# Cross-covariance attention on one core: two heads per step in 256-byte runs, or units of four heads in 1 KB runs with a written-out pipeline

## The chip, the cores and the metric

The kernel runs on one core of one Trainium2 chip. The number that is compared is the device time of one execution in microseconds (us), the median of several. The core has TensorE (matrix products, PE in the rows), VectorE (DVE), ScalarE (ACT), GpSimd (POOL), SyncE (SP, which here only issues DMAs), and 16 DMA engines that move data between HBM and the on-chip memory SBUF. TensorE writes its products to PSUM, which VectorE and ScalarE can read.

## What is computed

Q, K and V have the shape (8, 12, 512, 64): 96 heads, each of 512 tokens by 64 channels, in float32. The norms and the first product run over the tokens, so that the attention matrix of a head is only 64x64:

```python
Q_norm = Q / (np.linalg.norm(Q, axis=-2, keepdims=True) + 1e-10)
K_norm = K / (np.linalg.norm(K, axis=-2, keepdims=True) + 1e-10)
attn = np.einsum('bhnd,bhne->bhde', Q_norm, K_norm)
attn = np.exp(attn - np.max(attn, axis=-1, keepdims=True))
attn = attn / (np.sum(attn, axis=-1, keepdims=True) + 1e-10)
return np.einsum('bhnd,bhde->bhne', V, attn)
```

Both kernels leave out the subtraction of the maximum, since the logits are cosines. The three inputs and the output are 12.58 MB each, 50.33 MB in all.

## The kernel before, in words

The 512 tokens of a head are cut as (t p): token 128*t + p lies in partition p. So a partition holds, per head, four rows of 64 floats that lie 32 KB apart in HBM, and each run of contiguous bytes of a transfer is 256 B. The loop takes two heads per step, 48 steps. A step loads Q, K and V of two heads (three DMAs of 256 KB, lines 52 to 54) and casts them to bf16: VectorE writes Q and K side by side into `qkb` (lines 57 and 58), ScalarE casts V (line 60).

Then for each of the two heads: four matmuls with `qkb` as both operands accumulate the 128x128 Gram matrix of [Q K] (line 67). Its diagonal holds the squared norms of all 128 channels; the block of rows 0 to 63 and columns 64 to 127 holds the unscaled logits. VectorE takes the diagonal by a multiplication with the identity and a sum (line 71). ScalarE takes the square root (line 76), VectorE the reciprocal (line 78). TensorE transposes this column to a row (line 81), VectorE copies it (line 83), TensorE forms the outer product of the two halves of the row, a 64x64 matrix of scales (line 86), and VectorE multiplies the logits by it (lines 88 and 90). ScalarE takes the exponential with its row sums (line 93), VectorE the reciprocal of the sums (line 95) and the normalised bf16 matrix (line 97). Four transposes turn V (line 101), ScalarE copies them out of PSUM (line 103), four matmuls form the output (line 107) and VectorE copies it out (line 108). Behind the second head, one DMA stores both (line 110).

The square root and the exponential need different tables on ScalarE, and a table load stands in the instruction stream where they alternate. A planner orders the instructions by costs of its own; big tiles have two buffers, small ones three, and the PSUM tiles of lines 81, 86 and 107 have one. All DMAs, loads and stores, stand in SyncE's one queue in program order.

Of the kernel before, what the change touches and what calls it, by code (L numbers as in the profile page):

```python
# [1 line left out]

# [6 lines left out]

F32 = mybir.dt.float32  # L10
BF16 = mybir.dt.bfloat16
AF = mybir.ActivationFunctionType
ALU = mybir.AluOpType


@with_exitstack
def kernel(
    ctx: ExitStack,
    tc: tile.TileContext,
    Q: bass.AP,  # L20
    K: bass.AP,
    V: bass.AP,
    out: bass.AP,
):
    nc = tc.nc
    B, H, N, D = Q.shape
    assert D == 64 and N % 128 == 0
    NT = N // 128
    BH = B * H
    BB = 2  # L30

    Qf = Q.rearrange("b h (t p) d -> (b h) p t d", p=128)
    Kf = K.rearrange("b h (t p) d -> (b h) p t d", p=128)
    Vf = V.rearrange("b h (t p) d -> (b h) p t d", p=128)
    Of = out.rearrange("b h (t p) d -> (b h) p t d", p=128)

    const = ctx.enter_context(tc.tile_pool(name="const", bufs=1))
    ident = const.tile([128, 128], F32)
    make_identity(nc, ident)
    identb = const.tile([128, 128], BF16)  # L40
    nc.vector.tensor_copy(identb, ident)

    sb = ctx.enter_context(tc.tile_pool(name="sb", bufs=2))
    sb_small = ctx.enter_context(tc.tile_pool(name="sb_small", bufs=3))
    ps = ctx.enter_context(tc.tile_pool(name="ps", bufs=2, space=bass.MemoryType.PSUM))
    ps_sm = ctx.enter_context(tc.tile_pool(name="ps_sm", bufs=1, space=bass.MemoryType.PSUM))

    for bh0 in range(0, BH, BB):
        qf = sb.tile([128, BB, NT, 64], F32)
        kf = sb.tile([128, BB, NT, 64], F32)  # L50
        v = sb.tile([128, BB, NT, 64], F32)
        nc.sync.dma_start(out=qf, in_=Qf[bh0:bh0 + BB].rearrange("g p t d -> p g t d"))
        nc.sync.dma_start(out=kf, in_=Kf[bh0:bh0 + BB].rearrange("g p t d -> p g t d"))
        nc.sync.dma_start(out=v, in_=Vf[bh0:bh0 + BB].rearrange("g p t d -> p g t d"))

        qkb = sb.tile([128, BB, NT, 128], BF16)
        nc.vector.tensor_copy(qkb[:, :, :, 0:64], qf)
        nc.vector.tensor_copy(qkb[:, :, :, 64:128], kf)  # L58
        vb = sb.tile([128, BB, NT, 64], BF16)
        nc.scalar.copy(vb, v)  # L60

        so = sb.tile([128, BB, NT, 64], F32)

        for g in range(BB):
            gram = ps.tile([128, 128], F32)
            for i in range(NT):
                nc.tensor.matmul(gram, qkb[:, g, i, :], qkb[:, g, i, :], start=(i == 0), stop=(i == NT - 1))  # L67

            gi = sb_small.tile([128, 128], F32)
            nsq = sb_small.tile([128, 1], F32)  # L70
            nc.vector.tensor_tensor_reduce(  # L71
                out=gi, in0=gram, in1=ident, scale=1.0, scalar=0.0,
                op0=ALU.mult, op1=ALU.add, accum_out=nsq,
            )
            nrm = sb_small.tile([128, 1], F32)
            nc.scalar.sqrt(nrm, nsq)  # L76
            invn = sb_small.tile([128, 1], F32)
            nc.vector.reciprocal(invn, nrm)  # L78

            invnT_p = ps_sm.tile([1, 128], F32)  # L80
            nc.tensor.transpose(invnT_p, invn, ident)  # L81
            invnT = sb_small.tile([1, 128], F32)
            nc.vector.tensor_copy(invnT, invnT_p)  # L83

            scale2 = ps_sm.tile([64, 64], F32)
            nc.tensor.matmul(scale2, invnT[0:1, 0:64], invnT[0:1, 64:128])  # L86
            attn_raw = sb_small.tile([64, 64], F32)
            nc.vector.tensor_copy(attn_raw, gram[0:64, 64:128])  # L88
            attn = sb_small.tile([64, 64], F32)
            nc.vector.tensor_mul(attn, attn_raw, scale2)  # L90

            rsum = sb_small.tile([64, 1], F32)
            nc.scalar.activation(attn, attn, AF.Exp, accum_out=rsum)  # L93
            rinv = sb_small.tile([64, 1], F32)
            nc.vector.reciprocal(rinv, rsum)  # L95
            attnb = sb_small.tile([64, 64], BF16)
            nc.vector.tensor_scalar(attnb, attn, rinv, None, op0=ALU.mult)  # L97

            vt_p = ps.tile([64, NT, 128], BF16)
            for i in range(NT):  # L100
                nc.tensor.transpose(vt_p[:, i, :], vb[:, g, i, :], identb)  # L101
            vt = sb.tile([64, NT, 128], BF16)
            nc.scalar.copy(vt, vt_p)  # L103

            po = ps_sm.tile([128, NT, 64], F32)
            for i in range(NT):
                nc.tensor.matmul(po[:, i, :], vt[:, i, :], attnb)  # L107
            nc.vector.tensor_copy(so[:, g, :, :], po)  # L108

        nc.sync.dma_start(out=Of[bh0:bh0 + BB].rearrange("g p t d -> p g t d"), in_=so)  # L110


# [1 line left out]
_INS = ['Q', 'K', 'V']  # L114
_OUTS = [((8, 12, 512, 64), 'float32')]


# [23 lines left out]
```

## Time and profile before

| | |
|---|---|
| median of 3 runs | 349.55 us (349.44 to 349.60) |
| span of the profiled execution, first to last instruction | 347.9 us |
| median less this span | 1.65 us |
| busy: ScalarE / TensorE / VectorE / GpSimd | 247.0 / 209.6 / 193.3 / 0.7 us |
| busy share of the 16 DMA engines | 71.7% |
| DMA traffic | 50.34 MB in packets of 256 B, mean 145 GB/s |

The profiled execution has no time of its own beside its span; the 1.65 us are what the timed runs take outside the first and last instruction. Busy time is time in which the engine executed something. None of the shares says alone what sets the end; for that the profile has a chain of waits, followed back from the last instruction, and lists of who waited for whom.

### The profile page before, as it was taken

The page shows a single profiled execution, that of the slowest core. Times are in us where ns is not written, and L with a number is a line of the kernel's source. Part 1 is how long each engine was busy: PE and PEld are TensorE (multiplying, and loading weights), DVE is VectorE, ACT ScalarE, POOL GpSimd, SP SyncE. Part 2 cuts the span into 40 slices and gives each one's busy share as a digit, 9 for nine tenths or more (in the row PEclk, how much of TensorE's full clock was granted, in tenths as well). Part 3 has the DMA queues.
Part 4 walks back from the last instruction along what each step waited for, and adds up shares of the span by engine and source line. Part 5 has one row for each costly group of instructions (what it writes and reads, how often), then busy time and mean ns, then how long its engine had stood idle before and what let it go on. Part 6 is the DMA issues. An engine that isn't in the chain of part 4 may idle for free.

```text
span 347.9 us, 4965 instructions
## 1 busy us (share of the span) xinstructions
PE 209.6 (60%) x1440; PEld 133.9 (38%) x1440; DVE 193.3 (56%) x961; ACT 247.0 (71%) x529; POOL 0.7 (0%) x6
## 2 busy tenths in 40 slices
PE   2866656567556656665655764675566565576463
PEld 1534334334334334443433433443334343344242
DVE  2765556555556555645655555655565565465553
ACT  4887768758767786685875877668677687677763
POOL 0000000000000000000000000000000000000000
DMA  9787697498668768669748876786965984787642
GB/s 176 136 170 143 136 187 141 95 188 170 124 133 163 168 134 159 131 129 194 152 92 170 167 148 121 157 167 134 180 121 121 190 168 100 157 166 159 123 90 60
DMA packets 199706, 50.65 MB, mean 146 GB/s; under 512 B 199680, under 2 KB 199680, under 8 KB 199680
## 3 DMA queue, kind: packets, MB, share of 16 engines
q1 hardware_dynamic: 199680, 50.34, 71.7%
q8 instruction: 11, 0.18, 0.2%
q14 instruction: 15, 0.12, 0.1%
HBM read 37.75 MB, written 12.58 MB: 145 GB/s over the span
## 4 chain that ended last, share of the span: by engine, by line
PE 44%; DVE 31%; ACT 12%; issue 10%; DMA 1%; SPq 0%; ACTq 0%
PE vt_p L101 12%; DVE so L108 10%; PE po L107 9%; PE invnT_p L81 8%; PE scale L86 8%; PE gram L67 7%; ACT L93 5%; DVE gi L71 5%; ACT vt L103 4%; DVE attnb L97 3%; DVE rinv L95 3%; DVE qkb L58 2%; DVE attn_raw L88 2%; DVE invnT L83 2%; ACT attn L93 2%
## 5 line engine op out<-in xcount | busy, mean ns | idle before, releaser
L103 ACT COPY vt<-vt_p 64x512 bf16<-64x512 bf16 x96 | 54.1, 574 | 50.1 <-PE vt_p L101 50.1
L107 PE MATMUL po<-attnb,vt 64*128 64x64 bf16 x384 | 35.7, 230 | 70.2 <-DVE rinv L95 47.4
L67 PE MATMUL gram<-qkb 128*128 128x128 bf16 x384 | 52.1, 310 | 25.3 <-DVE qkb L58 25.3
L93 ACT ACT_TABLE_LOAD x48 | 61.6, 1283 | 2.4 <-DVE attn L90 1.6
L76 ACT ACT_TABLE_LOAD x48 | 61.6, 1283 | 0.9
L101 PE MATMUL vt_p<-identb,vb 128*64 128x128 bf16 x384 | 56.3, 313 | 0.4 <-DVE nsq L71 0.4
L107 PEld LDWEIGHTS <-vt 64*128 64x128 bf16 x384 | 23.3, 115 | 86.2 <-ACT attn L93 56.0
L108 DVE COPY so<-po 128x256 f32<-128x256 f32 x96 | 40.6, 423 | 26.9 <-PE po L107 25.3
L81 PE MATMUL invnT_p<-ident,invn 128*1 128x128 f32 x96 | 35.8, 373 | 29.4 <-DVE invn L78 29.4
L90 DVE TENSOR_TENSOR attn<-attn_raw,scale 64x64 f32<-64x64 f32 x96 | 20.5, 213 | 57.1 <-PE scale L86 56.7
L86 PE MATMUL scale<-invnT 1*64 1x64 f32 x192 | 45.3, 337 | 9.2 <-DVE invnT L83 8.9
L67 PEld LDWEIGHTS <-qkb 128*128 128x128 bf16 x384 | 37.1, 139 | 33.7 <-DVE qkb L58 31.2
L101 PEld LDWEIGHTS <-vb 128*64 128x64 bf16 x384 | 38.7, 163 | 16.3 <-issue 10.3
L76 ACT ACTIVATE nrm<-nsq 128x1 f32<-128x1 f32 x96 | 19.1, 201 | 29.1 <-DVE nsq L71 27.9
L83 DVE COPY invnT<-invnT_p 1x128 f32<-1x128 f32 x96 | 26.7, 278 | 22.0 <-PE invnT_p L81 16.0
L86 PEld LDWEIGHTS scale<-invnT 1*64 1x64 f32 x192 | 27.3, 201 | 29.4 <-DVE invnT L83 21.5
L71 DVE CUSTOM_DVE_ANT_0 gi<-gram,ident 128x128 f32<-128x128 f32 x96 | 27.5, 286 | 17.0 <-PE gram L67 16.8
L60 ACT CAST vb<-v 128x512 bf16<-128x512 f32 x48 | 28.9, 602 | 4.4 <-DMA v<-in_V_dram 4.4
L93 ACT ACTIVATE attn<-attn 64x64 f32<-64x64 f32 x96 | 24.0, 250 | 8.3 <-DVE attn L90 7.8
L95 DVE RECIPROCAL rinv<-rsum 64x1 f32<-64x1 f32 x96 | 14.3, 149 | 19.7 <-ACT attn L93 19.7
L81 PEld LDWEIGHTS invnT_p<-ident,invn 128*1 128x1 f32 x96 | 7.6, 79 | 44.4 <-DVE invn L78 37.6
L97 DVE TENSOR_SCALAR attnb<-attn,rinv 64x64 bf16<-64x64 f32 x96 | 23.4, 244 | 2.2
(14 smaller groups left out, 100.2 us busy)
## 6 DMA issues: line engine op xcount, KB each, us to landing
qf<-in_Q_dram SPq DMA_DIRECT2D x48, 256.0 KB, 4.5
kf<-in_K_dram SPq DMA_DIRECT2D x48, 256.0 KB, 4.3
v<-in_V_dram SPq DMA_DIRECT2D x48, 256.0 KB, 4.2
out_dram<-so SPq DMA_DIRECT2D x48, 256.0 KB, 3.0
```

Source lines behind the costliest of these rows:

```text
L67: nc.tensor.matmul(gram, qkb[:, g, i, :], qkb[:, g, i, :], start=(i == 0), stop=(i == NT - 1))
L71: nc.vector.tensor_tensor_reduce(out=gi, in0=gram, in1=ident, scale=1.0, scalar=0.0, op0=ALU.mult, op1=ALU.add, accum_out=nsq,)
L76: nc.scalar.sqrt(nrm, nsq)
L81: nc.tensor.transpose(invnT_p, invn, ident)
L83: nc.vector.tensor_copy(invnT, invnT_p)
L86: nc.tensor.matmul(scale2, invnT[0:1, 0:64], invnT[0:1, 64:128])
L93: nc.scalar.activation(attn, attn, AF.Exp, accum_out=rsum)
L97: nc.vector.tensor_scalar(attnb, attn, rinv, None, op0=ALU.mult)
L101: nc.tensor.transpose(vt_p[:, i, :], vb[:, g, i, :], identb)
L103: nc.scalar.copy(vt, vt_p)
L107: nc.tensor.matmul(po[:, i, :], vt[:, i, :], attnb)
L108: nc.vector.tensor_copy(so[:, g, :, :], po)
```

## The change

The kernel is written anew round units of four heads (24 units; a unit is two pairs, PU = 2).

- **Layout.** Tokens are cut as (p t): token 4*p + t lies in partition p. A partition's four rows of a head are then contiguous in HBM, in runs of 1 KB. Each load or store moves four heads, 512 KB. Q and K of the same token still meet in the same partition, and the sums over tokens don't depend on their order.
- **Order.** The planner is switched off and instructions are issued as written. In step s SyncE issues the loads of unit s + 3 and the store of unit s - 6; the compute engines do the Gram matrices and norms of unit s, logits and exponentials of s - 1, the transposes of V of s, the casts of s + 1, the normalisation of s - 1, the scaling of s, the outputs of s - 2. Loads have five buffers, outputs ten. The last four stores stand behind the loop.
- **Casts.** All on VectorE, five per unit. In every second head Q and K change places in `qkb`, so that Q of an even head and Q of the odd one lie in different halves.
- **Norms.** Four masked sums over the PSUM blocks per unit give one column of squared norms for the 128 Q channels of a pair and one for the K channels. GpSimd raises them to the power -0.5 in one instruction on 128x4 values: no square root on ScalarE, no reciprocal, no transposed norms.
- **Logits.** K's factor is a per-partition scalar on the K-by-Q blocks (`scale_k`, which also zeroes the other blocks); a float32 matmul with two stacked identities transposes them to Q-by-K for two heads at a time; Q's factor is the scale of the exponential.
- **Output.** The normalised matrices of two heads stand as a block diagonal 128x128 matrix, V is transposed for two heads at a time, and one matmul gives two heads for 128 tokens: eight per unit. ScalarE copies the transposed V and the outputs out of PSUM.

The diff, without the lines removed:

```diff
--- before.py
+++ after.py
@@ -4,13 +4,17 @@
 import concourse.tile as tile
 from concourse import bass_utils, mybir
 from concourse._compat import with_exitstack
...
 from concourse.masks import make_identity
 F32 = mybir.dt.float32
 BF16 = mybir.dt.bfloat16
 AF = mybir.ActivationFunctionType
 ALU = mybir.AluOpType
+D = 64
+T = 4
+HU = 4
+PU = HU // 2
 @with_exitstack
@@ -23,91 +27,184 @@
     out: bass.AP,
 ):
     nc = tc.nc
...
+    B, H, N, _ = Q.shape
+    assert N == 128 * T and Q.shape[3] == D
     BH = B * H
...
+    U = BH // HU
+    Qf = Q.rearrange("b h (p t) d -> p (b h) t d", p=128)
+    Kf = K.rearrange("b h (p t) d -> p (b h) t d", p=128)
+    Vf = V.rearrange("b h (p t) d -> p (b h) t d", p=128)
+    Of = out.rearrange("b h (p t) d -> p (b h) t d", p=128)
+    ctx.enter_context(tc.manual_schedule())
     const = ctx.enter_context(tc.tile_pool(name="const", bufs=1))
...
+    qp = ctx.enter_context(tc.tile_pool(name="qp", bufs=5))
+    vp = ctx.enter_context(tc.tile_pool(name="vp", bufs=5))
+    vbp = ctx.enter_context(tc.tile_pool(name="vbp", bufs=3))
+    qkp = ctx.enter_context(tc.tile_pool(name="qkp", bufs=4))
+    vtp = ctx.enter_context(tc.tile_pool(name="vtp", bufs=4))
+    sop = ctx.enter_context(tc.tile_pool(name="sop", bufs=10))
+    small = ctx.enter_context(tc.tile_pool(name="small", bufs=4))
+    ps_g = ctx.enter_context(tc.tile_pool(name="ps_g", bufs=2, space=bass.MemoryType.PSUM))
+    ps_v = ctx.enter_context(tc.tile_pool(name="ps_v", bufs=2, space=bass.MemoryType.PSUM))
+    ps_l = ctx.enter_context(tc.tile_pool(name="ps_l", bufs=2, space=bass.MemoryType.PSUM))
+    ps_o = ctx.enter_context(tc.tile_pool(name="ps_o", bufs=2, space=bass.MemoryType.PSUM))
+    LOAD_AHEAD = 3
+    CAST_AHEAD = 1
+    STORE_LAG = 6
+    qf, kf, vf, vb, qkb, gram, nsq, kqs, rq, lg, ex, ab, vt, so = ({} for _ in range(14))
+    def load_qk(u):
+        qf[u] = qp.tile([128, HU, T, D], F32, name="qf")
+        kf[u] = qp.tile([128, HU, T, D], F32, name="kf")
+        nc.sync.dma_start(out=qf[u], in_=Qf[:, u * HU:(u + 1) * HU])
+        nc.sync.dma_start(out=kf[u], in_=Kf[:, u * HU:(u + 1) * HU])
+    def load_v(u):
+        vf[u] = vp.tile([128, HU, T, D], F32, name="vf")
+        nc.sync.dma_start(out=vf[u], in_=Vf[:, u * HU:(u + 1) * HU])
+    def store(u):
+        nc.sync.dma_start(out=Of[:, u * HU:(u + 1) * HU], in_=so[u])
+    def casts(u):
+        t_ = qkb[u] = qkp.tile([128, HU, T, 2 * D], BF16, name="qkb")
+        nc.vector.tensor_copy(t_[:, 0::2, :, 0:D], qf[u][:, 0::2])
+        nc.vector.tensor_copy(t_[:, 1::2, :, D:2 * D], qf[u][:, 1::2])
+        nc.vector.tensor_copy(t_[:, 0::2, :, D:2 * D], kf[u][:, 0::2])
+        nc.vector.tensor_copy(t_[:, 1::2, :, 0:D], kf[u][:, 1::2])
+        w = vb[u] = vbp.tile([128, T, HU, D], BF16, name="vb")
+        nc.vector.tensor_copy(w.rearrange("p t h d -> p h t d"), vf[u])
+    def grams(u):
+        g = gram[u] = ps_g.tile([128, PU, 4, D], F32, name="gram")
+        for h in range(HU):
+            o = g[:, h // 2, 2 * (h % 2):2 * (h % 2) + 2, :]
+            for t in range(T):
+                x = qkb[u][:, h, t, :]
+                nc.tensor.matmul(o, x, x, start=(t == 0), stop=(t == T - 1))
+    def norms(u):
+        n2 = nsq[u] = small.tile([128, 2, PU], F32, name="nsq")
+        for p in range(PU):
+            for c, (blk, m) in enumerate(((gram[u][:, p, 0::3, :], mask_q), (gram[u][:, p, 1:3, :], mask_k))):
+                scr = small.tile([128, 2, D], F32, name="scr")
+                nc.vector.tensor_tensor_reduce(
+                    out=scr, in0=blk, in1=m, scale=1.0, scalar=1e-20,
+                    op0=ALU.mult, op1=ALU.add, accum_out=n2[:, c, p:p + 1],
+                )
+        r = rq[u] = small.tile([128, 2, PU], F32, name="rq")
+        nc.gpsimd.tensor_tensor(out=r, in0=n2, in1=mhalf, op=ALU.pow)
+    def scale_k(u):
+        kk = kqs[u] = small.tile([128, PU, 2, D], F32, name="kqs")
+        for p in range(PU):
+            nc.vector.scalar_tensor_tensor(
+                out=kk[:, p], in0=gram[u][:, p, 0::3, :], scalar=rq[u][:, 1, p:p + 1], in1=off_diag,
+                op0=ALU.mult, op1=ALU.mult,
+            )
+    def logits(u):
+        l = lg[u] = ps_l.tile([128, PU, D], F32, name="lg")
+        for p in range(PU):
+            nc.tensor.matmul(l[:, p, :], kqs[u][:, p].rearrange("p a d -> p (a d)"), eye2)
+    def exps(u):
+        e = ex[u] = small.tile([128, PU, D], F32, name="ex")
+        s = small.tile([128, PU], F32, name="esum")
+        for p in range(PU):
+            nc.scalar.activation(e[:, p, :], lg[u][:, p, :], AF.Exp, scale=rq[u][:, 0, p:p + 1], accum_out=s[:, p:p + 1])
+        ex[u] = (e, s)
+    def normalise(u):
+        e, s = ex[u]
+        ri = small.tile([128, PU], F32, name="rinv")
+        nc.vector.reciprocal(ri, s)
+        a = ab[u] = small.tile([128, PU, 2, D], BF16, name="ab")
+        for p in range(PU):
+            nc.vector.scalar_tensor_tensor(
+                out=a[:, p], in0=e[:, p, None, :].to_broadcast([128, 2, D]), scalar=ri[:, p:p + 1], in1=on_diag,
+                op0=ALU.mult, op1=ALU.mult,
+            )
+    def vtrans(u):
+        for p in range(PU):
+            ps = ps_v.tile([128, T, 128], BF16, name="vps")
+            for t in range(T):
+                nc.tensor.transpose(ps[:, t, :], vb[u][:, t, 2 * p:2 * p + 2, :].rearrange("p h d -> p (h d)"), identb)
+            w = vtp.tile([128, T, 128], BF16, name=f"vt{p}")
+            nc.scalar.copy(w, ps)
+            vt[u, p] = w
+    def outs(u):
+        s = so[u] = sop.tile([128, HU, T, D], F32, name="so")
+        for p in range(PU):
+            po = ps_o.tile([128, T, 2, D], F32, name="po")
+            for t in range(T):
+                nc.tensor.matmul(po[:, t], vt[u, p][:, t, :], ab[u][:, p].rearrange("p a d -> p (a d)"))
+            nc.scalar.copy(s[:, 2 * p:2 * p + 2].rearrange("p h t d -> p t h d"), po)
+    for u in range(LOAD_AHEAD):
+        load_qk(u)
+        load_v(u)
+    ident = const.tile([128, 128], F32, name="ident")
     make_identity(nc, ident)
...
+    identb = const.tile([128, 128], BF16, name="identb")
+    nc.gpsimd.tensor_copy(identb, ident)
+    mask_q = ident.rearrange("p (a d) -> p a d", a=2)
+    swap = const.tile([128, 2, D], F32, name="swap")
+    nc.gpsimd.tensor_copy(swap[:, 0, :], ident[:, D:])
+    nc.gpsimd.tensor_copy(swap[:, 1, :], ident[:, :D])
+    mask_k = swap
+    eye2 = const.tile([128, D], F32, name="eye2")
+    nc.gpsimd.tensor_tensor(out=eye2, in0=ident[:, :D], in1=ident[:, D:], op=ALU.add)
+    blocks = const.tile([128, 3, D], F32, name="blocks")
+    nc.gpsimd.memset(blocks, 0.0)
+    nc.gpsimd.memset(blocks[0:D, 1, :], 1.0)
+    nc.gpsimd.memset(blocks[D:, 0, :], 1.0)
+    nc.gpsimd.memset(blocks[D:, 2, :], 1.0)
+    off_diag = blocks[:, 0:2, :]
+    on_diag = blocks[:, 1:3, :]
+    mhalf = const.tile([128, 2, PU], F32, name="mhalf")
+    nc.gpsimd.memset(mhalf, -0.5)
+    for u in range(CAST_AHEAD):
+        casts(u)
+    for s in range(U + 2):
+        if s + LOAD_AHEAD < U:
+            load_qk(s + LOAD_AHEAD)
+            load_v(s + LOAD_AHEAD)
+        if 0 <= s - STORE_LAG:
+            store(s - STORE_LAG)
+        if s < U:
+            grams(s)
+            norms(s)
+        if 0 <= s - 1 < U:
+            logits(s - 1)
+            exps(s - 1)
+        if s < U:
+            vtrans(s)
+        if s + CAST_AHEAD < U:
+            casts(s + CAST_AHEAD)
+        if 0 <= s - 1 < U:
+            normalise(s - 1)
+        if s < U:
+            scale_k(s)
+        if 0 <= s - 2 < U:
+            outs(s - 2)
+    for u in range(U + 2 - STORE_LAG, U):
+        store(u)
 # ---- launch: one core; inputs and outputs as the reference has them ----
```

## Rows read from the trace of the kernel before

**Rows 1.** Page, part 1: busy time, share of the span and instructions of each engine.
```profile
PE 209.6 (60%) x1440; PEld 133.9 (38%) x1440; DVE 193.3 (56%) x961; ACT 247.0 (71%) x529; POOL 0.7 (0%) x6
```
**Rows 2.** Page, part 4: the chain that ended last, shares of the span by engine.
```profile
PE 44%; DVE 31%; ACT 12%; issue 10%; DMA 1%; SPq 0%; ACTq 0%
```
**Rows 3.** Waits: who waited for whom, us in total, times, longest us.
```profile
DVE attn L90 <- PE scale L86: 56.7, 93, 1.1
PEld L107 <- ACT attn L93: 56.0, 45, 1.7
```
**Rows 4.** Groups on ScalarE: shapes xcount | busy us, mean ns | idle before, releasers.
```profile
L93 ACT ACT_TABLE_LOAD x48 | 61.6, 1283 | 2.4 <-DVE attn L90 1.6
L103 ACT COPY vt<-vt_p 64x512 bf16<-64x512 bf16 x96 | 54.1, 574 | 50.1 <-PE vt_p L101 50.1
...
L93 ACT ACTIVATE attn<-attn 64x64 f32<-64x64 f32 x96 | 24.0, 250 | 8.3 <-DVE attn L90 7.8
...
L93 ACT ACTIVATION_READ_ACCUMULATOR attn<-attn 64x1 f32 x96 | 17.9, 186 | 0.0
```
**Rows 5.** Page, part 3: DMA queue, packets, MB, share of 16 engines.
```profile
q1 hardware_dynamic: 199680, 50.34, 71.7%
q8 instruction: 11, 0.18, 0.2%
```
**Rows 6.** DMA packets of the stretch 4 to 12 us, loads alone.
```profile
DMA packets 6917, 1.74 MB, mean 218 GB/s; under 512 B 6917, under 2 KB 6917, under 8 KB 6917
```
**Rows 7.** DMA rate of the stretch 30 to 34 us in 40 slices.
```profile
GB/s 287 287 289 287 292 289 287 241 225 215 213 225 215 215 228 207 223 210 202 192 182 126 108 90 41 18 0 0 0 0 0 0 0 0 0 0 0 0 0 72
```
**Rows 8.** DMA queues of 195.97 to 196.47 us: one packet alone.
```profile
DMA packets 1, 0.01 MB, mean 16 GB/s; under 512 B 0, under 2 KB 0, under 8 KB 0
...
q14 instruction: 1, 0.01, 3.8%
```
**Rows 9.** DMA queues of 174.39 to 174.89 us: another packet alone.
```profile
q8 instruction: 1, 0.02, 12.9%
```
**Rows 10.** Groups on VectorE, columns as in rows 4.
```profile
L71 DVE CUSTOM_DVE_ANT_0 gi<-gram,ident 128x128 f32<-128x128 f32 x96 | 27.5, 286 | 17.0 <-PE gram L67 16.8
...
L97 DVE TENSOR_SCALAR attnb<-attn,rinv 64x64 bf16<-64x64 f32 x96 | 23.4, 244 | 2.2
...
L57 DVE CAST qkb<-qf 128x512 bf16<-128x512 f32 x48 | 19.4, 404 | 4.4 <-DMA qf<-in_Q_dram 4.4
...
L95 DVE RECIPROCAL rinv<-rsum 64x1 f32<-64x1 f32 x96 | 14.3, 149 | 19.7 <-ACT attn L93 19.7
...
L71 DVE DVE_READ_ACCUMULATOR2_ANT nsq<- 128x1 f32 x96 | 7.9, 82 | 0.0
```
**Rows 11.** Timeline, 5 to 14 us: start us, us, engine line op xcount, idle before.
```profile
5.19 0.43 DVE L58 CAST qkb<-kf 128x512 bf16<-128x512 f32 x1 [0.77 <-DMA kf<-in_K_dram]
...
5.67 1.03 PE L67 MATMUL gram<-qkb 128*128 128x128 bf16 x8 [5.67 <-DVE qkb L58]
...
13.04 0.42 DVE L108 COPY so<-po 128x256 f32<-128x256 f32 x1
13.38 0.42 DVE L57 CAST qkb<-qf 128x512 bf16<-128x512 f32 x1
```
**Rows 12.** Groups on TensorE, columns as in rows 4.
```profile
L86 PE MATMUL scale<-invnT 1*64 1x64 f32 x192 | 45.3, 337 | 9.2 <-DVE invnT L83 8.9
...
L86 PEld LDWEIGHTS scale<-invnT 1*64 1x64 f32 x192 | 27.3, 201 | 29.4 <-DVE invnT L83 21.5 <-issue 5.7 <-DVE invn L78 2.2
```
**Rows 13.** Groups on GpSimd, columns as in rows 4.
```profile
masks.py:199 POOL TENSOR_SCALAR_AFFINE_SELECT ident<-ident 128x128 f32<-128x128 f32 x1 | 0.3, 292 | 0.1
```
**Rows 14.** Timeline, 0 to 1 us and the last instruction.
```profile
0.74 0.43 SPq L52 DMA_DIRECT2D qf<-in_Q_dram  x1
...
344.53 0.38 SPq L110 DMA_DIRECT2D out_dram<-so  x1
```
**Rows 15.** DMA rate of the stretch 0 to 5 us in 40 slices.
```profile
GB/s 0 0 0 0 0 0 0 0 0 0 0 0 0 0 16 119 141 100 145 219 279 291 287 289 283 287 287 291 287 274 231 225 197 225 229 223 217 223 227 215
```

More of the change, by code (lines that the diff above doesn't have):

```diff
@@ L25 @@
     nc = tc.nc
-    B, H, N, D = Q.shape
-    assert D == 64 and N % 128 == 0
-    NT = N // 128
+    B, H, N, _ = Q.shape
+    assert N == 128 * T and Q.shape[3] == D
     BH = B * H
[L30 to L35, printed above, removed]
-    const = ctx.enter_context(tc.tile_pool(name="const", bufs=1))
@@ L38 @@
-    ident = const.tile([128, 128], F32)
-    make_identity(nc, ident)
[L40 to L110, printed above, removed]
```

1 line of the change is left out of this document (removed).

## The prediction, made before the changed kernel was run

> **What bounds the kernel now.** I read the shares first. ScalarE is busiest with 71%, TensorE 60%, VectorE 56% [rows 1], the DMA engines 71.7% [rows 5]: none is full, so the time is made of waits. The chain of waits confirms it: TensorE 44%, VectorE 31%, ScalarE 12%, issue 10%, DMA 1% [rows 2]. The reader is to see that the end hangs on a chain that goes from engine to engine inside one head, and not on one resource. The waits name its links: VectorE for the outer product on TensorE (56.7 us), TensorE for the exponential on ScalarE (56.0 us) [rows 3]. Behind the second lies the table load: 48 loads of 1.283 us for the exponential [rows 4], and as many for the square root, 123 us of ScalarE's 247.
>
> So after a rewrite that overlaps units, the question is which resource fills first. I work out each per unit of four heads, 24 units, against the span of 347.9 us; the median is 1.65 us above it.
>
> **DMA.** The 50.33 MB stay, the packet goes from 256 B to 1 KB. No row shows a 1 KB packet, so it is bounded. Loads alone run at 218 GB/s [rows 6], with the engines full: 13.6 B/ns on each of 16, or 18.8 ns a packet. One packet of 8 KB alone (16 GB/s over 0.5 us) takes 3.8% of 16 x 0.5 us, 0.304 us [rows 8]: 26.9 B/ns, 38 ns per KB. Then of 18.8 ns, 9.5 are bytes and 9.3 are fixed. A 1 KB packet is 38 + 9.3 = 47.3 ns, 346 GB/s, 145 us for everything. The ends: with the best rate of 256 B packets, 287 GB/s [rows 7], the fixed part is 4.8 ns and the total 131 us; with no fixed part 117 us; at the rate of the 16 KB packets (11 make 0.18 MB [rows 5]; one alone takes 12.9% of 8 us, 1.03 us [rows 9]) 64 ns per KB, 198 us; with a cost in proportion to bytes, so no gain at all, 231 us. I take 145, because the row at 218 is the sustained one and three quarters of the traffic are loads. First bytes move at 1.75 us [rows 15], and the issue at 0.74 [rows 14] stays first in SyncE's queue.
>
> The page "DMA: Bandwidth & Descriptors" of the Trainium skill (Specifications) puts line rate at 512 B and more, some 27 GiB/s an engine. By that the sum would be about 116 us, and DMA would bound nothing; the 8 KB packet agrees with the engine's rate (26.9 B/ns), and no row here shows whether 1 KB reaches it.
>
> Does anything keep the queue from being fed? SyncE's queue in step s: two loads, V's load, the store of s - 6. The loads wait for casts(s - 2), which freed the buffers, so they run up to five units ahead (a cast of step s - 3); the outputs of s - 6 that the store needs come in step s - 4, so the store adds no wait to the loads queued behind it. 96 issues, 0.38 to 0.43 us each when nothing holds them [rows 14], are 40 us. I count the queue as full from 1.75 us on.
>
> **VectorE per unit.** Four casts of 512 values, 0.404 each [rows 10]: 1.62. V's cast, which comes over from ScalarE, has 1024 values: between 0.404 and 0.81; the slope from the 64-value row (0.244) to the 512-value one is 0.36 ns a value, so 0.6. Four masked sums of 128x128 with their accumulator reads, 0.286 + 0.082 [rows 10]: 1.47. Two `scale_k` over 128 values of PSUM, as the masked sum: 0.57. One reciprocal 0.149. Two normalisations of 128 values, between 0.244 and 0.286: 0.54. Sum 4.95. Instructions with no wait between them overlap by 0.08 us (0.42 long, 0.34 apart [rows 11]); 18 of them give at most 1.4, I take half: 4.3. Waits: sixteen Gram matmuls take twice 1.03 us [rows 11] from the last Q/K cast, and beside them lie V's cast, the normalisation and `scale_k`, 1.86 less overlap, so 0.2 to 0.5. Makes 4.6 to 4.9; with a hand-over more, **5.0 us a unit**.
>
> **TensorE per unit.** 16 Gram, 8 transposes, 8 outputs, each 128 columns at 0.13 us [rows 11]: 4.1, less 0.2 or so for every stream's last latency, 3.5. The float32 logit matmuls come as two instructions each (192 for 96) [rows 12]; two of those serially, load and product (0.201 + 0.337), are 1.1 per pair at most, 0.34 x 2 at least: 1.4 to 2.2 for two pairs. About 5.0, at worst 6.3, beside VectorE.
>
> **ScalarE per unit.** Copies of 512 values 0.574, four: 2.3; two exponentials 0.250 + 0.186 [rows 4]: 0.9. 3.2, so 76 us; of 97 table loads one stays. The 123 us go for good, nothing takes their place there.
>
> **GpSimd.** One power on 128x4 values a unit. No row shows a power. Below: next to nothing. Above: nothing in the trace limits it. The nearest row on the engine is 0.292 us for 128x128 [rows 13], and I take that order, 0.3 to 1 us. What hides it: between the norms and `scale_k` VectorE has five casts and a normalisation, 1.62 + 0.6 + 0.69 = 2.9 us. Beyond 2.9 us each microsecond lands on every unit.
>
> **The ends by compute.** Q, K and V of unit 0 (1.57 MB at 346 GB/s) land at 1.75 + 4.5 + 0.8 = 7.0, first casts done at 7.6. The constants on GpSimd, a few of 0.3 us, lie under that. Then 23 units. Behind the last cast: Gram 2.0, norms 1.5, power 0.7, `scale_k` 0.6, logits 1.0, exponential 0.6, normalisation 0.7, outputs and copies 1.9: 9. Then the last store: 3.4 us from issue to the end now, 344.53 against 347.9 [rows 14]. 7.6 + 23 x 5.0 + 9 + 3.4 = 135 us.
>
> **The sum.** A unit is 2.1 MB, 6.1 us of DMA at 346 GB/s, against 5.0 of compute. DMA is later. It starts at 1.75, moves 145, and its last store lands about 1.5 later: 148, and a microsecond for gaps: 149. The tail fits: when the last load lands, ten stores (5.2 MB, 15 us) are still out, more than the 9 us of compute behind it. With 1.65: **151 us**, by 199 faster.
>
> **The rivals.**
>
> *Power on GpSimd exposed* (0.2). Waits land between norms and `scale_k`. For it: five casts in a row stand there, and nobody has timed the power. Against: 2.9 us of cover. With a power of 3 us that gets going only behind the casts (2.2 us), `scale_k` waits about 2.3 us in each unit: P = 7.3, 7.6 + 168 + 12.4 = 188, with 1.65 190; with a power of 1.5 us P = 5.8 and DMA still hides it. So 160 to 195.
> The page "SBUF — State Buffer" of the Trainium skill (Who interferes with whom) is the rule that speaks for it: a cast in a two-port mode and a GpSimd instruction exclude each other for a whole instruction. That GpSimd is locked out no row here shows, since it works only at the start.
>
> *DMA at the engine's rate* (0.2). If the fixed part is small, 117 to 131 us of DMA, compute is last: 135 + 1.65 = 137, 130 to 141. For it: the 8 KB packet; against: the sustained 218.
>
> *Packets cost by the byte* (0.06). 231 us of DMA: 235 to 238. For it: at 256 B the engines reach 287 for a while [rows 7], loads alone too [rows 15], so part of the 18.8 ns may be no fixed cost but a slower path that longer packets meet as well; against: the 8 KB packet.
>
> *Slower than before* (0.02). A power so long that it sets the period: P over (347.9 - 20) / 23 = 14.3 us, and as 2.1 us of the unit (norms, `scale_k`) lie outside it, a power over 12 us, forty times the 0.292 row. From there on it is slower than 349.6. Against: only four values per partition.
>
> **How the numbers follow.** Forecast (DMA bound, 141 to 160) 0.5, the others as given, 0.02 for what I don't see. The range 133 to 190 leaves out the packets by the byte, the slower case and small parts of two others, somewhat under 2 in 10. Runs of before lie within 0.16 us; 0.2% (0.7 us) is what a measurement can tell from no change. All cases but one are far on the fast side: faster 0.97, same 0.01, slower 0.02.
>
> **What would show it.** Right: DMA share near 100% from 2 us to the end, 330 to 370 GB/s, the last chain through loads and stores, VectorE busy 100 to 120 us, ScalarE 70 to 85 with one table load, VectorE's longest waits on DMA. Wrong: DMA share under 85% with VectorE waiting on GpSimd at `scale_k` (first rival), VectorE or TensorE over 85% and DMA idle in between (second), DMA full at under 250 GB/s (third). TensorE's logit instructions over 0.55 us each would put TensorE in VectorE's place.

## The result, and the profile after

The changed kernel takes **145.05 us** (144.59 to 145.51, four runs) against 349.56: a ratio of 0.415, with a 95% interval of 0.414 to 0.416. Forecast were 151 us, in a range from 133 to 190. The profiled execution took 145.51 us, its span is 143.1, so 2.4 us lie around it. The kernel before was executed 32 times in all: 31 executions took 349.26 to 349.77 us and one took 326.28, of which no trace was kept, so its cause is open.

The page's first part, which answers to [rows 1]:

```profile
PE 95.3 (67%) x864; PEld 83.7 (59%) x864; DVE 100.9 (71%) x432; ACT 64.8 (45%) x193; POOL 29.9 (21%) x39
```

No compute engine is over 71%, as before. What has changed is the DMA: the busy share and the rate in 40 slices of 3.6 us, then the queue, which answers to [rows 5]. Its share adds up the times of all packets, so it passes 100% where packets of one engine overlap:

```profile
DMA  4999999999999999999999999999999999999993
GB/s 133 336 353 349 348 348 351 350 348 348 348 350 348 376 370 378 368 371 384 368 372 380 372 376 379 371 380 371 375 369 369 371 382 372 382 377 386 377 322 113
...
q1 hardware_dynamic: 50688, 50.34, 104.5%
```

The reader is to see three things: the 9 from the second slice to the last but one; the step from 349 to about 375 GB/s in the 14th slice, where the first store joins the loads; and no gap. A rate that is flat at two levels, whatever the engines do, is the mark of transfers that wait for nobody; the first experiment tests that. The chain of waits [rows 2] now says the same, by engine and by line:

```profile
DMA 65%; DVE 14%; SPq 12%; PE 2%; ACT 1%; issue 1%; ACTq 0%
DMA vf<-in_V_dram 59%; DMA qf<-in_Q_dram 6%; SPq L65 5%; DVE vb L84 4%; SPq L66 4%; DVE ab L134 4%; SPq L70 3%; DVE scr L100 3%; DVE kqs L111 2%; PE lg L119 2%; ACT ex L125 1%; DVE rinv L131 1%; PE po L153 0%; ACT so L154 0%; DVE qkb L78 0%
```

DMA was 1% of it and is 65%. From the waits, VectorE's (total, times, longest):

```profile
DVE vb L84 <- DMA vf<-in_V_dram: 15.2, 24, 2.8
DVE qkb L80 <- DMA kf<-in_K_dram: 11.6, 17, 1.4
DVE qkb L78 <- DMA qf<-in_Q_dram: 5.1, 2, 4.3
```

The last V of a unit is late in every one of 24 units. GpSimd's power appears as nobody's cause. The groups on which terms of the sum rested (mean ns before the last bar):

```profile
L105 POOL TENSOR_TENSOR rq<-nsq,mhalf 128x4 f32<-128x4 f32 x24 | 27.6, 1151 | 102.0 <-DVE nsq L100 102.0
...
L119 PE MATMUL lg<-eye,kqs 128*128 128x64 f32 x96 | 22.8, 381 | 19.4 <-DVE kqs L111 19.3
L119 PEld LDWEIGHTS lg<-eye,kqs 128*128 128x128 f32 x96 | 18.8, 271 | 24.9 <-DVE kqs L111 24.9
...
L84 DVE CAST vb<-vf 128x1024 bf16<-128x1024 f32 x24 | 16.7, 694 | 15.2 <-DMA vf<-in_V_dram 15.2
...
L145 ACT ACT_TABLE_LOAD x1 | 1.3, 1283 | 0.7 <-PEq L222 0.7
```

### The profile page after: what moved, and what is told of

Its sections match the earlier page's. It is cut to its first block, busy times and chain, and to the rows that moved or that the text cites. A ratio compares the mean times of both kernels' runs of the same rounds, so it can differ in the third digit from the quotient of the medians.

```text
span 143.1 us, 2715 instructions
## 1 busy us (share of the span) xinstructions
PE 95.3 (67%) x864; PEld 83.7 (59%) x864; DVE 100.9 (71%) x432; ACT 64.8 (45%) x193; POOL 29.9 (21%) x39
## 4 chain that ended last, share of the span: by engine, by line
DMA 65%; DVE 14%; SPq 12%; PE 2%; ACT 1%; issue 1%; ACTq 0%
DMA vf<-in_V_dram 59%; DMA qf<-in_Q_dram 6%; SPq L65 5%; DVE vb L84 4%; SPq L66 4%; DVE ab L134 4%; SPq L70 3%; DVE scr L100 3%; DVE kqs L111 2%; PE lg L119 2%; ACT ex L125 1%; DVE rinv L131 1%; PE po L153 0%; ACT so L154 0%; DVE qkb L78 0%
## 5 line engine op out<-in xcount | busy, mean ns | idle before, releaser
L105 POOL TENSOR_TENSOR rq<-nsq,mhalf 128x4 f32<-128x4 f32 x24 | 27.6, 1151 | 102.0 <-DVE nsq L100 102.0
L92 PEld LDWEIGHTS <-qkb 128*128 128x128 bf16 x384 | 33.8, 130 | 25.3 <-DVE qkb L80 24.6
L119 PE MATMUL lg<-eye,kqs 128*128 128x64 f32 x96 | 22.8, 381 | 19.4 <-DVE kqs L111 19.3
L119 PEld LDWEIGHTS lg<-eye,kqs 128*128 128x128 f32 x96 | 18.8, 271 | 24.9 <-DVE kqs L111 24.9
L145 ACT COPY vt<-vps 128x512 bf16<-128x512 bf16 x48 | 25.7, 593 | 8.7 <-PE vps L143 8.7
L154 ACT COPY so<-po 128x512 f32<-128x512 f32 x48 | 26.4, 618 | 0.3 <-PE po L153 0.3
L143 PE MATMUL vps<-identb,vb 128*128 128x128 bf16 x192 | 20.9, 274 | 1.9 <-DVE vb L84 1.9
L153 PE MATMUL po<-ab,vt 128*128 128x128 bf16 x192 | 20.9, 274 | 0.6 <-DVE ab L134 0.6
L143 PEld LDWEIGHTS <-vb 128*128 128x128 bf16 x192 | 19.3, 138 | 2.2 <-DVE vb L84 2.2
L80 DVE CAST qkb<-kf 128x512 bf16<-128x512 f32 x24 | 10.2, 424 | 11.6 <-DMA kf<-in_K_dram 11.6
L78 DVE CAST qkb<-qf 128x512 bf16<-128x512 f32 x24 | 10.2, 425 | 5.1 <-DMA qf<-in_Q_dram 5.1
L79 DVE CAST qkb<-qf 128x512 bf16<-128x512 f32 x24 | 10.1, 420 | 0.0
L81 DVE CAST qkb<-kf 128x512 bf16<-128x512 f32 x24 | 10.1, 419 | 0.0
```

Source lines behind the costliest of these rows:

```text
L92: nc.tensor.matmul(o, x, x, start=(t == 0), stop=(t == T - 1))
L105: nc.gpsimd.tensor_tensor(out=r, in0=n2, in1=mhalf, op=ALU.pow)
L119: nc.tensor.matmul(l[:, p, :], kqs[u][:, p].rearrange("p a d -> p (a d)"), eye2)
L143: nc.tensor.transpose(ps[:, t, :], vb[u][:, t, 2 * p:2 * p + 2, :].rearrange("p h d -> p (h d)"), identb)
L145: nc.scalar.copy(w, ps)
L153: nc.tensor.matmul(po[:, t], vt[u, p][:, t, :], ab[u][:, p].rearrange("p a d -> p (a d)"))
```

## The experiments

Theory A: the transfers alone set the time after, at a price per packet of a fixed part and a part by the byte. Theory B: the compute chain still sets it, by when it frees the buffers that loads wait for. Times are medians; spans are those of the profiled execution.

### Transfers without computation: 1 KB, 256 B, 4 KB

Everything behind the loads is left out, and V's buffer is stored. V has 12 buffers here instead of 5, since each is now held until its store is done:

```diff
-        nc.sync.dma_start(out=Of[:, u * HU:(u + 1) * HU], in_=so[u])
+        nc.sync.dma_start(out=Of[:, u * HU:(u + 1) * HU], in_=vf[u])
```

For 256 B the tokens are cut (t p); for 4 KB a unit's 2048 rows are cut as one block, 16 to a partition.

1 KB, expected: 

> Leaves out all computation: the same loads and stores in the same order with the same 1 KB runs, and the output is V. Theory A (the transfers alone set the changed kernel's time): span 139 to 143 us, loads alone near 349 GB/s, with stores near 375, within 3 us of the changed kernel's 143.1. Theory B (the compute chain holds the loads back by when it frees their buffers): clearly shorter, 118 to 133 us.

256 B, expected: 

> Leaves out all computation, the output is V; runs of 256 B as in the kernel before. Theory A with a fixed part per packet (9 ns of 18.8): loads at 218 GB/s, loads with stores up to 287, 195 to 231 us in all. If the packet size cost nothing, as with e1_dma_1k. Either way well under the 347.9 us of the kernel before, whose chain of engines set its time.

4 KB, expected: 

> Leaves out all computation, the output is V; runs of 4 KB. With 38 ns per KB (the 8 KB packet of the trace) and a fixed 9 ns per packet, 161 ns per 4 KB, 407 GB/s, 124 us, span about 127. If 1 KB is already at line rate, no change against e1_dma_1k.

Spans: 141.4, 220.1 and 125.9 us (143.3, 221.9 and 127.6 with what lies around). The rates in 40 slices, in this order:

```profile
GB/s 138 334 344 352 347 349 348 348 348 348 348 348 348 373 370 385 374 375 382 373 381 377 374 385 372 374 385 373 376 383 373 381 378 374 385 374 385 385 385 115
```
```profile
GB/s 158 218 218 218 218 217 218 218 218 217 218 218 217 248 222 256 241 232 256 234 239 255 225 245 246 228 255 238 235 257 230 243 253 220 254 247 226 215 215 166
```
```profile
GB/s 143 333 390 422 416 410 409 413 407 409 414 407 407 422 414 420 419 414 420 416 415 420 415 420 419 415 418 416 416 422 414 416 419 416 418 418 420 420 418 151
```

The first is the changed kernel's line almost slice for slice: all its computation costs 1.7 us of span (143.1 against 141.4). Theory A holds, B falls. And the loads give the price of a packet on each of 16 engines at the sustained rate: 256 x 16 / 218 = 18.8 ns, 1024 x 16 / 348 = 47.1, 4096 x 16 / 409 = 160.2. From the last two, 37.7 ns per KB and 9.4 fixed; that gives 18.8 for 256 B, which is what was measured. One straight line through three sizes.

### Computation without most transfers

```diff
+        if u >= 5:
+            qf[u], kf[u] = qf[u - 5], kf[u - 5]
+            return
```

and the same for V; the loads of units 5 to 23 are left out.

> Leaves out the loads of units 5 to 23, which compute again on the first five units' data; everything else as in the changed kernel. Theory A: the compute engines need 4.3 to 5.0 us a unit, span 118 to 135 us, clearly under 143. Theory B: the time stays at 140 to 143 us.

Span 116.9 us (118.8). VectorE is full; busy time of PE, PEld, DVE, ACT and POOL in a stretch, with granted clock and DMA share:

```profile
40.00:60.00 20.00, 13.79 (x180) 11.50 (x180) 19.82 (x91) 13.03 (x41) 5.92 (x6) 1.00 0.40 134
60.00:80.00 20.00, 13.83 (x180) 11.55 (x180) 19.82 (x91) 13.03 (x41) 5.92 (x6) 1.00 0.39 131
```

19.82 of 20 us, and a unit every 4.03 us (the power starts at 59.20 and 63.23). So the computation alone would end 26 us sooner, and the limit behind the transfers is VectorE.

### One part undone, one part alone

The changed kernel with 256 B runs, and the kernel before with 1 KB runs; each edit of the source is the cut of the tokens and nothing else:

```diff
-    Qf = Q.rearrange("b h (p t) d -> p (b h) t d", p=128)
+    Qf = Q.rearrange("b h (t p) d -> p (b h) t d", p=128)
```

> The changed kernel with tokens cut as (t p), so runs of 256 B; nothing else differs. Theory A (the transfers set the time): it falls back to the time of its transfers alone, 220 to 224 us span, loads at 218 GB/s. If the packet size is not what counts: 143 us.

> The kernel before with tokens cut as (p t), so runs of 1 KB; nothing else differs. Theory A (before, the chain of engines set the time): 335 to 349 us, with the DMA share down from 72% to about 45%. If the transfers counted before as well: under 300 us.

The first: 224.3 us span (226.4; ratio 0.648, 0.646 to 0.650), the transfers' 220.1 and 4 more. Of the 204 us gained, 81 hang on the length of the runs, once the rest is there.

The second: 319.7 us (321.5; ratio 0.920, 0.917 to 0.922), a miss, the gain is twice what I allowed at most. The queue, TensorE's wait for the casts (25.3 us in 35 waits before), and two groups, to be read beside [rows 4] and [rows 10]:

```profile
q1 hardware_dynamic: 52224, 50.34, 51.2%
...
PE gram L67 <- DVE qkb L58: 5.2, 2, 4.7
...
L93 ACT ACT_TABLE_LOAD x45 | 57.7, 1283 | 0.8
...
L57 DVE CAST qkb<-qf 128x512 bf16<-128x512 f32 x48 | 20.4, 424 | 36.4 <-PE gram L67 28.7 <-DMA qf<-in_Q_dram 7.6 <-DMA v<-in_V_dram 0.2
```

A load of Q lands 2.8 us after its issue where it took 4.5, and TensorE's wait for the casts is 20 us shorter. That looks as if the loads had come late before, but the two traces speak against it. In the kernel before, the casts of Q and K began 2.4 us after their load had landed (median of 96, by the landings in the trace; 3 of them within 0.3 us). And VectorE's idle time that ended with a load of Q has not shrunk: 7.6 us, against 4.4 before [rows 10].

What did change beside the runs is the order. The source differs in the layout alone, but the planner ordered the instructions anew: the exponential's table is loaded 45 times in place of 48, and VectorE casts Q and K of a step directly one behind the other from the 16th step on, where the kernel before has 1 to 7 other instructions between them. The clock is no rival, since eight Gram products take 1.03 us in both. So the 28 us belong to this edit as it was built; how much of them is the runs and how much the new order, no run separates. The kernel before itself, at 256 B and in its own order, has the one execution of 326.28 us.

### The power on GpSimd, three and six times

```diff
+        for i in range(5):
+            r0 = small.tile([128, 2, PU], F32, name=f"rx{i}")
+            nc.gpsimd.tensor_tensor(out=r0, in0=n2, in1=mhalf, op=ALU.pow)
```

> The power on GpSimd is done three times, and only the last is used: 3.45 us a unit in place of 1.15. Theory A: the transfers pace a unit at 5.5 us, in which 4.1 us lie between the norms and scale_k, so nothing changes: span 142.5 to 144.5. If the power is already exposed: 2 x 1.15 x 24 = 55 us more, about 198.

> The power six times, 6.9 us a unit. Now it must show: the unit is 6.9 us plus the 1.4 us of norms and scale_k that lie outside the cover, 8.3 to 8.5 us, so 7.6 + 23 x 8.4 + 12 = 205 to 220 us. If GpSimd and the casts shut each other out for whole instructions, some 2 us a unit more: 250 us.

Three: span 142.4 us (145.27, ratio 0.4155): the time does not move, though VectorE now waits for GpSimd ten times, 5.4 us in all. Six: 201.8 us (204.3). Now VectorE waits for GpSimd at `scale_k`, and the groups give the time of a power:

```profile
DVE kqs L114 <- POOL rq L108: 86.0, 24, 4.8
...
L106 POOL TENSOR_TENSOR rx<-nsq,mhalf 128x4 f32<-128x4 f32 x120 | 122.2, 1076 | 44.4 <-DVE nsq L100 44.4
L108 POOL TENSOR_TENSOR rq<-nsq,mhalf 128x4 f32<-128x4 f32 x24 | 24.0, 1001 | 0.0
```

The mechanism of the first rival is real, and its place too; at one power of 1.15 us it is far from deciding. The time came 3 us under the range because six powers take 6.1 us (122.2 / 24 + 24.0 / 24), not 6.9: the last ones, beside no cast, take 1.00.

### Stores four steps behind in place of six

```diff
-    STORE_LAG = 6
+    STORE_LAG = 4
```

> The changed kernel with stores four steps behind in place of six. Theory A: loads alone move at 349 GB/s and loads with stores at 375, so stores that begin some 9 us earlier save 9 x (375 - 349) / 375 = 0.6 us: span 141.5 to 143. If the late stores matter because an earlier store holds up the loads queued behind it: 146 us or more.

Span 143.2 us; 145.7 us, ratio 0.4166 (0.4159 to 0.4172) against 0.4149 (0.414 to 0.4158): no gain, if anything 0.4% slower, and neither of the two expectations came. The rate:

```profile
GB/s 141 315 347 349 348 348 353 346 348 348 359 382 374 372 382 373 375 375 371 373 383 375 375 377 373 384 373 379 357 362 377 379 378 374 377 377 385 284 243 216
```

The step up comes two slices sooner, as expected, and the last three slices fall to 284, 243 and 216 where the changed kernel has 377, 322 and 113. What stores save early they lack late: the stores kept back are what the DMA engines move while the last units are still computed. That is what the late stores are for; the lag of six against four is worth nothing net.

### Towards a faster kernel: Q and K in runs of 2 KB

The transfers bound the time and longer packets are cheaper per byte, so Q and K get eight tokens to a partition; a head then fills 64 partitions, two heads stand side by side. The Gram sums become products over 64 partitions, and the odd heads' [K Q] comes from a second copy of Q by ScalarE:

```diff
+    Qf = Q.rearrange("b h n d -> (b h n) d").rearrange("(g p t) d -> p g t d", p=128, t=2 * T)
...
+        nc.scalar.copy(t_[D:, :, :, 2, :], qf[u][D:])
...
+                    x = qkb[u][D * a:D * a + D, p, t, a:a + 2, :].rearrange("p c d -> p (c d)")
```

> Q and K in runs of 2 KB (eight tokens to a partition, a head in 64 partitions, two heads side by side), V and output as they are; Gram sums as 32 products over 64 partitions in place of 16 over 128, ScalarE makes a second copy of the odd heads' Q. Theory A (transfers): a 2 KB packet takes 2 x 38 + 9 = 85 ns, 385 GB/s for half of the bytes, 6.7 us less: span 135 to 138. Rival: 16 more products a unit, 1.2 us at full clock and 1.9 at half, put TensorE (3.0 to 3.9 us a unit now) over the 5.2 us that the transfers then take: 143 us or more.

> Both of the two together. Theory A: the gains add, span 134.5 to 137.5.

142.3 us by the ratio of 0.4069 (0.4051 to 0.4086; span 140.6), 143.7 by the median of six; with both edits 140.9 by 0.403 (0.402 to 0.404), and 143.0. Faster than the change, but both miss their range: the gain is less than half of what was expected. The single runs scatter from 140 to 146, so that the lag's own part stays open. The rate rose as expected, and fell early; under it one of TensorE's waits, which shows the reason:

```profile
GB/s 144 358 334 384 375 369 372 371 376 373 373 372 366 399 387 385 396 389 385 396 383 391 398 384 392 397 385 393 396 388 395 393 387 398 380 385 227 152 249 198
...
PE gram L90 <- ACT qkb L77: 25.0, 22, 1.5
```

The rival named TensorE, but for the wrong reason. TensorE is not full (93.9 us busy in the run, 95.3 in the changed kernel); it waits for ScalarE's copy, which stands behind two others in ScalarE's order. The 32 products are no load: at the upper clock, 31 of them take 1.06 us (70.78 to 71.84), where the changed kernel's 16 over 128 partitions take 1.18. So, moving that copy:

```diff
         if 0 <= s - 1 < U:
             logits(s - 1)
             exps(s - 1)
+        if s + CAST_AHEAD < U:
+            cast_odd(s + CAST_AHEAD)
         if s < U:
             vtrans(s)
```

> As e10_qk2k, with ScalarE's copy of the odd heads' Q ahead of the two copies of the transposed V instead of behind them, so the Gram products of the next unit start 1.07 us earlier. In e10_qk2k they waited 25 us in all for this copy, the compute fell behind the transfers, and the last stores came one by one behind it (150 to 250 GB/s in the last 14 us). If that was the cause: the transfers set the end again, 50.33 MB at about 385 GB/s after 1.75 us, span 134 to 137. If the loss at the end has another cause (the clock of TensorE, say): 139 to 141 as in e10_qk2k.

```profile
GB/s 133 374 363 385 374 373 368 372 376 375 372 376 363 399 390 386 395 388 389 390 391 400 383 394 397 388 393 396 389 399 380 392 400 388 391 385 385 356 301 123
```

Span 136.9 us; **139.3 us**, ratio 0.398 (0.397 to 0.399): beats both kernels, 4% under the changed one, and the transfers reach the end again. Of the 28.3 us that TensorE's weight loads waited for the copy, 5.0 are left.

## Why the prediction was right

**The bound.** Right: DMA at 346 GB/s from loads of 1 KB was the forecast, 348 to 349 is measured. The split of 18.8 ns into 9.3 fixed and 38 ns per KB came from one 8 KB packet alone [rows 8] beside the sustained rate [rows 6]; three sizes give 9.4 and 37.7. That the agreement is so close is in part luck: the prediction gives a reason for 218 against 287 GB/s, but none for the 8 KB packet against the 16 KB one [rows 9], by which the total would have been 198 us. Neither that packet's price nor the rate of 287 [rows 7] was met by the stream of loads. The Trainium skill's page "DMA: Bandwidth & Descriptors" (Specifications) has full rate from 512 B on; here 1 KB moves at 349 and 4 KB at 409 GB/s, so the measurement goes against it. The prediction's 116 us fit 27 GB/s an engine, not 27 GiB/s, by which the estimate would be 108; and the 8 KB packet's 26.9 B/ns lie 7% under 27 GiB/s.

**The term that was mis-sized.** 149 us of span were forecast and 143.1 came. Loads together with stores move at 375, not 346: the 35 MB behind the 46th microsecond take 93 us in place of 101. I had taken the sustained rate of loads for all of it. The 1.65 us around the span are 2.4 in the profiled execution.

**The compute.** 135 us by engines were forecast and 116.9 measured, with the bound on the right engine. VectorE's sum of 4.95 us a unit less half of the possible overlap, plus waits, gave 5.0. Measured, the instructions of a unit add up to 5.4: the two-block operations cost more (`scale_k` 0.344, not 0.286), the big cast 0.69, not 0.6. Their full overlap, 1.4, and no wait at all give 4.03. TensorE's logit instructions, 0.381 and 0.271 us, stay under the 0.55 at which it would have taken VectorE's place. ScalarE, 76 forecast, is 64.8, with one table load, as said.

**GpSimd.** The power takes 1.15 us, just over the guess of 0.3 to 1, under a cover that is some 3 us in the first units and 4.1 later, at the pace of the transfers. First rival: excluded at its price, shown as a mechanism with six powers. The rule of the Trainium skill's "SBUF — State Buffer" (Who interferes with whom) is weaker here than I priced it: the power takes 1.00 us behind the casts, 1.15 in the mean beside casts of 0.42, 1.65 in the 2 KB kernel beside casts of 0.69, while the casts keep their length:

```profile
L103 POOL TENSOR_TENSOR rq<-nsq,mhalf 128x4 f32<-128x4 f32 x24 | 39.6, 1649 | 89.3 <-DVE nsq L98 89.3
```

(the 2 KB kernel, before its copy was moved). The excess, 0.15 and 0.65 us, is at most one cast; GpSimd is not held up until all five are done, as the first rival had it.

**Second and third rival.** DMA at the engine's rate would have been 117 to 131 us: at 1 KB the transfers alone span 141, and only 4 KB runs, with 126, come into that range. Cost by the byte would have been 231: that is near the 220 of the 256 B runs, and 1 KB runs are far from it.

**What bounded the kernel before.** "Not on one resource" was right, and DMA at 1% of the chain [rows 2] agrees with loads that land 2.4 us ahead of their cast. The forecast of 335 to 349 us for that kernel with 1 KB runs was wrong, at 321.5. It took for granted that nothing but the runs would differ, while the planner's order differed too; what either is worth stays open.

## What to carry to other kernels

Price a new packet size from two rows of the old trace, one saturated stretch and one big packet alone: fixed part plus bytes. Then check it by running the transfers alone, since one lone packet can mislead: the 16 KB one would have given 198 us here. Once transfers are the bound, only the form of the transfers pays, longer runs above all, and an order that leaves stores to move while the last units are computed. Where a planner orders the instructions, an edit of the layout can change the order too: compare the two orders before you put a gain down to the transfers.

## What the runs showed of the hardware

**The granted clock.** TensorE's clock column reads 1.00 in every stretch of the kernel before, and in the changed kernel it goes up and down between its two levels, 2.4 and 1.2 GHz. Three stretches of the changed kernel (the clock is the third number from the end), and the sixteen Gram products in each:

```profile
6.00:24.00 18.00, 12.56 (x100) 11.24 (x101) 12.23 (x52) 5.38 (x16) 3.79 (x3) 1.00 1.08 347
25.00:35.00 10.00, 6.91 (x92) 5.95 (x91) 9.28 (x46) 5.96 (x21) 2.78 (x3) 1.00 1.10 349
35.60:40.60 5.00, 4.44 (x36) 4.18 (x37) 4.39 (x19) 2.70 (x9) 1.56 (x2) 0.50 1.10 348
```
```profile
17.36 1.89 PE L92 MATMUL gram<-qkb 128*128 128x128 bf16 x16 [0.52 <-DVE qkb L80]
...
31.13 1.18 PE L92 MATMUL gram<-qkb 128*128 128x128 bf16 x16 [0.52 <-DVE qkb L80]
...
35.63 1.89 PE L92 MATMUL gram<-qkb 128*128 128x128 bf16 x16 [0.52 <-DVE qkb L80]
```

1.18 us at 1.00 and 1.89 at 0.50; but 1.89 also in the first stretch, where the column says 1.00. Up to the first recorded change, at 25 us, the column shows full speed and the durations show half. The kernel before has no recorded change, and its eight products in 1.03 us [rows 11] fit the lower level: the changed kernel's eight transposes take 1.06 us at the lower (38.95) and 0.61 at the upper (43.09). So the kernel before ran at 1.2 GHz throughout, as far as durations tell. The clock rose at 25 us, after products that followed each other nearly unbroken from 21.0 us on, and fell at 35 us, after units in which TensorE stood idle for 0.5 and some 1.2 us; with most loads left out it stayed at 1.00 from 40 to 80 us. The end hardly depends on it: all the computation together costs 1.7 us of span.

**Loads and stores together** move more than loads alone, at each size: 375 against 349 GB/s at 1 KB, some 240 against 218 at 256 B, 418 against 409 at 4 KB.
